# Fifteen weight tiles of the second layer split earlier and kept in DRAM, and its last convolution blocks cut into halves of tokens

## The chip, the cores and the metric

The kernel runs on one core of one Trainium2 chip. The metric is the device time of one execution in microseconds (us), given as the median of several runs. A core has engines that run beside each other, each with an in-order queue of its own: TensorE (PE, with its weight loads listed as PEld), VectorE (DVE), ScalarE (ACT), GpSimd (POOL) and SyncE (SP, which here only issues transfers between DRAM and the core's SBUF). PE's sums go into PSUM.

## The reference, cut to what matters

Two blocks of a model work on 1024 tokens with 1024 channels. The first block has two layers: layer 0 mixes an attention with a pooling over windows of 2, 4, 8 and 16 tokens; layer 1 is a gated convolution of 31 taps along the tokens, each channel by itself. The change concerns the end of layer 0 and the first part of layer 1:

```python
def even_mixer(h, w_in, sinks, pool_w, pool_scale, w_out):          # layer 0
    proj = h @ w_in
...
    ya = sliding_window_attention(q, k, v, sinks).astype(h.dtype) * jax.nn.silu(ga)
    yb = multiscale_pool(u, pool_w, pool_scale) * jax.nn.silu(gb)
    return jnp.concatenate([ya, yb], axis=-1) @ w_out

def odd_mixer(h, w_in, dw_w, dw_b, ln_g, ln_b, w_out):              # layer 1
    proj = h @ w_in
    a, b, gate = jnp.split(proj, [CONV_WIDTH, 2 * CONV_WIDTH], axis=-1)
    glu = a * jax.nn.sigmoid(b)
    conv = lax.conv_general_dilated(
        glu, dw_w.astype(glu.dtype), window_strides=(1,), padding=[(CONV_K - 1, 0)],
        dimension_numbers=('NWC', 'WIO', 'NWC'), feature_group_count=CONV_WIDTH)
    cf = conv.astype(jnp.float32) + dw_b.astype(jnp.float32)
...
    y = jax.nn.silu(cn).astype(h.dtype) * jax.nn.silu(gate)
    return y @ w_out
```

Each layer normalises its input before, and its output after, and adds it to x.

## The kernel before, in words

All products are of float32 values that are split into two parts: a high half, rounded by ACT (`hi`, L382), and a low half, the value less its high half, by DVE (`lo`, L386). A product is three matmuls: high by high, high by low, low by high. So every weight tile of 128 x 1024 (512 KB) is loaded by SP into `wf`, copied by ACT into `wh`, and subtracted by DVE into `wl` (`weights`, `wtile`). These come from the pool `stream`, which has two buffers for each name. A tile is then used for 24 matmuls on each of two chunks of 512 tokens (`project_chunk`, L425); the chunks are `c0h`/`c0l` and `c1h`/`c1l`.

`layer0_pooling` projects 4 tiles of u and 4 tiles of gates. For each group POOL sums windows, DVE and ACT make `dh` and `dl`, PE multiplies them by the small pooling weights (L1100), and DVE scales. At its end, `ahead` splits the first columns of the output product's input, and loads `wo0` and `wo1`.

`mix_out(0)` is layer 0's output product: `load_wo` (L499) brings eight tiles `wo0` to `wo7` through `wf`, each split by ACT and DVE, in the order 0, 1, 2, 3, 7, 6, 5, 4; for each block t of 128 tokens PE multiplies (`out_project`, L510) in two halves, and ACT and DVE normalise (`finish`), load and store x (L682, L714), and build the chunks of layer 1. A table `hooks` can call a function after a block t.

`layer1_conv` projects, for each block j of 128 channels, tile 8 + j (b; ACT applies a sigmoid, `sg`, L1129) and tile j (a; DVE multiplies, `glu`, L1140), then eight gate tiles (`gt`, L1192, stored to DRAM). The convolution of a block is shared out: ON_POOL[j] = 12 of the 31 taps go by ACT and POOL (ACT scales a shifted copy, `tap`, L1154, POOL adds it to `side`, L1155), the other 19 by DVE (one accumulation each, L1161, into `acc`; ACT starts it, L1159), and DVE adds both into `y` (L1164). Block 0's first half of tokens is convolved by itself (`first`), its second half and all other blocks in operations of 512 and 1024 columns. `tap` has three buffers, `acc` two, in PSUM.

Then `mix_out(1)` begins, with the class `Conv`: for each block of tokens PE transposes y (L109), DVE takes statistics, ACT normalises (`z`, L121), PE transposes back (L132), ACT applies the silu (`s`, L135), DVE multiplies by the gate, and the result is split into `yh` and `yl`.

A scheduler decides the order of the instructions on each engine, from the order in which the code asks for them and their dependences; the order printed below is what it made. Every engine works off its own order strictly.

Of the kernel before, what the change touches and what calls it, by code (L numbers as in the profile page):

```python
# [8 lines left out]
F32 = mybir.dt.float32  # L9
F32R = mybir.dt.float32r  # L10
# [5 lines left out]
S = 1024  # L16
D = 1024
NT = S // 128
KD = D // 128
# [3 lines left out]
EPS_B = 1e-5  # L23
BIG = 1e30
CONV_K = 31
ON_POOL = [12] * 8
GATES = [0] * 6 + [2000] * 2
EARLY = 0
HA, HB = 2, 5
# [302 lines left out]
class Kernel:  # L332
    def __init__(self, ctx, tc, a, out):
        self.tc, self.nc, self.a, self.out = tc, tc.nc, a, out
        self.const = ctx.enter_context(tc.tile_pool(name="const", bufs=1))
        self.stream = ctx.enter_context(tc.tile_pool(name="stream", bufs=2))
        self.small = ctx.enter_context(tc.tile_pool(name="small", bufs=4))
        edge = ctx.enter_context(tc.tile_pool(name="edge", bufs=1, side="right"))
        edge.tile([128, 56], F32, name="edge")
        self.const.tile([128, 32], F32, name="even")  # L340
        self.pp = ctx.enter_context(tc.tile_pool(name="pp", bufs=1, space=PSUM))
        self.px = {}

    def pool(self, name, side="left", bufs=1):
        g = self.tc.tile_pool(name=name, bufs=bufs, side=side, reuse_waits="tile")
# [54 lines left out]
    def weights(self, src, shape, hold=None):  # L400
# [8 lines left out]
        self.lo(l, f, h)  # L409
        return h, l  # L410

    def wtile(self, name, i, hold=None):
        return self.weights(self.a[name][i], [128, KD, 128], hold)

    def project(self, w, chunks, consume, m=128):
# [110 lines left out]
    def run(self):  # L526
# [22 lines left out]
        y = yp[1].tile([128, KD, S], F32, name="y")  # L549
        self.eps = EPS_A  # L550
        self.layer0_attention(chunks, y)
        early = self.pool("e0", "right")
        mixed = Feature(self, y)
        mixed.open(early[1])
# [2 lines left out]
        def ahead():  # L557
# [1 line left out]
            self.load_wo(early[1], a["wo0"], mixed.order[:EARLY_WO], wo)  # L559
            mixed.first(1)  # L560

        self.layer0_pooling(chunks, y, ahead)
        self.close(hp1, hp0)

        chunks, hp = self.mix_out(
            0, mixed, a["x"], self.x1, a["wo0"],
            a["post_norm"][0:1, :], a["pre_norm"][1:2, :], EPS_A, [(0, 4), (4, 8)], 0, wo=wo,
        )
        self.close(early)
        mixed = Conv(self, y)  # L570
        self.layer1_conv(chunks, y)
        self.close(*hp)
# [479 lines left out]
                )  # L1052
            nc.gpsimd.tensor_tensor(out=ym, in0=ym, in1=sg[:, c], op=ALU.mult)

    def layer0_pooling(self, chunks, y, ahead):
        nc, a = self.nc, self.a
        pb = self.pool("pool0", "right", 2)
        pool = pb[1]
        psc = pool.tile([128, 4], F32, name="psc", bufs=1)
        nc.sync.dma_start(out=psc, in_=a["psc"])  # L1060
        nc.vector.tensor_scalar(out=psc, in0=psc, scalar1=0.5, scalar2=None, op0=ALU.mult)
        cnt = pool.tile([128, 4, 16], F32, name="cnt", bufs=1)
        nc.sync.dma_start(out=cnt, in_=a["cnt"])
        pwf = pool.tile([128, 4, 128], F32, name="pwf", bufs=1)
        nc.sync.dma_start(out=pwf, in_=a["pw"])
        pwh = pool.tile([128, 4, 128], F32R, name="pwh", bufs=1)
        pwl = pool.tile([128, 4, 128], F32R, name="pwl", bufs=1)
        self.hi(pwh, pwf)
        self.lo(pwl, pwf, pwh)
        for g in (3, 2, 1, 0):  # L1070
            self.project(
                self.wtile("w0", 10 + g), chunks, lambda p, l0, n: self.scaled0(y[:, 4 + g, l0:l0 + n], p, l0, n)
            )
        for g in (3, 2, 1, 0):
            win = 2 << g
            if g == 0:
                ahead()
            sg = pool.tile([128, S], F32, tag="sg", name="sg")
            self.project(self.wtile("w0", 14 + g), chunks, lambda p, l0, n: self.silu2(pool, sg, p, l0, n))
            u = y[:, 4 + g, :]  # L1080
            w, step = u, 1
            while step < win:
                nw = pool.tile([128, S], F32, tag="win", name="win")
                nc.gpsimd.tensor_copy(out=nw[:, :step], in_=w[:, :step])
                nc.gpsimd.tensor_tensor(out=nw[:, step:], in0=w[:, step:], in1=w[:, :S - step], op=ALU.add)
                w, step = nw, 2 * step
            edge = self.small.tile([128, 16], F32, tag="edge", name="edge", bufs=2)
            nc.vector.tensor_tensor(out=edge, in0=w[:, :16], in1=cnt[:, g, :], op=ALU.mult)
            nc.vector.tensor_tensor(out=u[:, :16], in0=edge, in1=u[:, :16], op=ALU.subtract)
            nc.vector.scalar_tensor_tensor(  # L1090
                out=u[:, 16:], in0=w[:, 16:], scalar=1.0 / win, in1=u[:, 16:], op0=ALU.mult, op1=ALU.subtract
            )
            dh = pool.tile([128, S], F32R, tag="dh", name="dh")
            dl = pool.tile([128, S], F32R, tag="dl", name="dl")
            self.hi(dh, u)
            self.lo(dl, u, dh)
            for c in range(2):
                p = self.ps()
                for j, (st, mv) in enumerate(((pwh, dh), (pwh, dl), (pwl, dh))):
                    nc.tensor.matmul(out=p, lhsT=st[:, g, :], rhs=mv[:, HALF[c]], start=(j == 0), stop=(j == 2))  # L1100
                nc.vector.scalar_tensor_tensor(
                    out=u[:, HALF[c]], in0=p, scalar=psc[:, g:g + 1], in1=sg[:, HALF[c]],
                    op0=ALU.mult, op1=ALU.mult,
                )
        self.close(pb)
# [3 lines left out]
    def layer1_conv(self, chunks, y):  # L1109
# [36 lines left out]
        def conv(j, c0, n, acc, side, tap_tile):  # L1146
            glu = glus[j]
            for i in range(ON_POOL[j]):
                src, w = glu[:, c0 + i:c0 + i + n], dw[:, j, i:i + 1]
                if i == 0:  # L1150
                    nc.scalar.activation(out=side, in_=src, func=AF.Identity, scale=w, bias=dwb[:, j:j + 1])
                else:
                    tap = tap_tile()
                    nc.scalar.activation(out=tap, in_=src, func=AF.Copy, scale=w)  # L1154
                    nc.gpsimd.tensor_tensor(out=side, in0=side, in1=tap, op=ALU.add)  # L1155
            for i in range(ON_POOL[j], CONV_K):
                src, w = glu[:, c0 + i:c0 + i + n], dw[:, j, i:i + 1]
                if i == ON_POOL[j]:
                    nc.scalar.activation(out=acc, in_=src, func=AF.Copy, scale=w)  # L1159
                else:  # L1160
                    nc.vector.scalar_tensor_tensor(  # L1161
                        out=acc, in0=src, scalar=w, in1=acc, op0=ALU.mult, op1=ALU.add
                    )
            nc.vector.tensor_tensor(out=y[:, j, c0:c0 + n], in0=acc, in1=side, op=ALU.add)  # L1164
# [4 lines left out]
        def side_tile():  # L1169
            return pool.tile([128, S], F32, tag="side", name="side")  # L1170
# [26 lines left out]
            for c in HALF:  # L1197
                nc.scalar.dma_start(out=self.gates[:, j, c], in_=gt[:, c])
        xp = self.psum_pool("pxc1", "acc")
        for j in range(KD):  # L1200
            c0 = N if j == 0 else 0
            n = S - c0
            acc = xp[1].tile([128, S], F32, tag="acc", name="acc", bufs=2)
            conv(j, c0, n, acc[:, :n], side_tile()[:, :n], lambda: tap_tile()[:, :n])
        self.close(low, mid, top, xp)


# [656 lines left out]
```

## Time and profile before

| | us |
|---|---|
| median of 3 runs | 1967.2 (1966.25 to 1968.06) |
| the profiled execution | 1961.58 |
| its span, first to last instruction | 1959.8 |
| PE busy in the span | 1902.9 (97%) |
| DVE busy | 1340.1 (68%) |
| ACT busy | 905.8 (46%) |
| POOL busy | 538.3 (27%) |

The mean granted clock of PE is 0.992 of full speed over the span. The shares are means over stages that differ much: POOL is nearly idle in most of the program and full in the convolution. 1.8 us of the profiled execution lie outside the span. The profiled execution is one of its own, and is shorter than the median of the timed runs by 5.6 us.

### The profile page before, as it was taken

What the parts mean: (1) busy time and instruction counts of PE and PEld (TensorE: products, weight loads), DVE (VectorE), ACT (ScalarE), POOL (GpSimd) and SP (SyncE); (2) the same over time, 40 slices, a digit from 0 to 9 for tenths busy, and PEclk for the clock granted to TensorE, in tenths of its full rate; (3) what the DMA queues carried; (4) which work ended last, traced back from release to release, by engine and by line L of the source; (5) the groups of instructions that cost most, each with busy time, mean ns of one, the idle gap of its engine ahead of it and who ended that gap; (6) DMA issues with size and microseconds to landing.
All of it is one profiled execution on the core that took longest, in us unless ns stands there. A gap on an engine that the chain in (4) does not pass through costs nothing. (4 is left out here: it accounts for less than half of the span.)

```text
span 1959.8 us, 25557 instructions
## 1 busy us (share of the span) xinstructions
PE 1902.9 (97%) x9584; PEld 1615.4 (82%) x9584; DVE 1340.1 (68%) x2045; ACT 905.8 (46%) x1577; POOL 538.3 (27%) x433
## 2 busy tenths in 40 slices
PE   7999999899999899999999999999999999999998
PEld 6888788787778678898999999787888887888886
DVE  7788656699898565565656665657767665665666
ACT  6556234456665665555444543424333333333333
POOL 4122602479998121001010201202433230000002
PEclk9999999999999999999999999999999999999999
DMA  4110143111122642101110202522544446653654
GB/s 152 59 40 32 62 132 118 44 54 44 43 76 91 221 120 68 54 34 55 44 55 33 81 33 73 205 94 81 172 167 142 156 158 214 222 204 118 215 193 172
DMA packets 122747, 212.15 MB, mean 108 GB/s; under 512 B 9576, under 2 KB 59112, under 8 KB 122624
## 3 DMA queue, kind: packets, MB, share of 16 engines
q1 hardware_dynamic: 120320, 206.34, 31.2%
q10 hardware_dynamic: 2304, 4.20, 0.6%
q8 instruction: 75, 1.23, 0.3%
q14 instruction: 48, 0.39, 0.1%
HBM read 156.46 MB, written 54.03 MB: 107 GB/s over the span
## 5 line engine op out<-in xcount | busy, mean ns | idle before, releaser
L1155 POOL TENSOR_TENSOR side<-side,tap 128x1024 f32<-128x1024 f32 (+1 forms) x99 | 235.6, 2386 | 24.9 <-ACT tap L1154 17.8
L1161 DVE SCALAR_TENSOR_TENSOR acc<-glu,dw,acc 128x1024 f32<-128x1024 f32 (+1 forms) x162 | 193.9, 1239 | 11.5 <-ACT acc L1159 10.2
L425 PE MATMUL pj<-c0h,wl 128*128 128x512 f32 (+1 forms) x496 | 187.9, 379 | 5.7 <-DVE wl L386 5.7
L425 PE MATMUL pj<-c0h,wh 128*128 128x512 f32 (+1 forms) x496 | 189.1, 381 | 4.2 <-ACT gt L1192 2.7
L425 PE MATMUL pj<-c0l,wh 128*128 128x512 f32 (+1 forms) x496 | 187.6, 378 | 0.0
L425 PE MATMUL pj<-c1h,wh 128*128 128x512 f32 (+1 forms) x496 | 176.5, 356 | 3.6 <-ACT sg L1129 1.8
L425 PE MATMUL pj<-c1l,wh 128*128 128x512 f32 (+1 forms) x496 | 177.1, 357 | 0.0
L425 PE MATMUL pj<-c1h,wl 128*128 128x512 f32 (+1 forms) x496 | 176.8, 357 | 0.0
L1154 ACT ACTIVATE tap<-glu,dw 128x1024 f32<-128x1024 f32 (+1 forms) x99 | 103.8, 1055 | 78.9 <-POOL side L1155 78.4
L382 ACT ACTIVATE ah<-act 128x1024 fp32r<-128x1024 f32 x56 | 59.2, 1060 | 168.4 <-issue 82.2
L386 DVE TENSOR_TENSOR al<-act,ah 128x1024 fp32r<-128x1024 f32 x56 | 68.5, 1225 | 90.7 <-ACT ah L382 90.6
L382 ACT ACTIVATE ph<-pt 128x512 fp32r<-128x512 f32 (+3 forms) x144 | 72.8, 516 | 104.8 <-PE pt L1461 68.3
L386 DVE TENSOR_TENSOR pl<-pt,ph 128x512 fp32r<-128x512 f32 (+3 forms) x144 | 83.3, 587 | 41.0 <-ACT ph L382 40.6
L425 PEld LDWEIGHTS pj<-c0h,wl 128*128 128x128 f32 x496 | 94.1, 190 | 19.0 <-DVE wl L386 6.1
L425 PEld LDWEIGHTS pj<-c0h,wh 128*128 128x128 f32 x496 | 94.1, 190 | 18.3 <-ACT gt L1192 3.1
L425 PEld LDWEIGHTS pj<-c1h,wh 128*128 128x128 f32 x496 | 94.2, 190 | 17.9 <-ACT sg L1129 2.3
L386 DVE TENSOR_TENSOR wl<-wf,wh 128x1024 fp32r<-128x1024 f32 (+1 forms) x66 | 90.7, 1374 | 23.4 <-ACT wh L382 23.2
L425 PEld LDWEIGHTS pj<-c1l,wh 128*128 128x128 f32 x496 | 94.3, 190 | 13.0 <-DVE c1l L386 0.4
L425 PEld LDWEIGHTS pj<-c1h,wl 128*128 128x128 f32 x496 | 94.5, 190 | 12.3
L425 PEld LDWEIGHTS pj<-c0l,wh 128*128 128x128 f32 x496 | 93.9, 189 | 12.6 <-issue 0.2
L1715 PE MATMUL pd<-bh,ah 128*128 128x512 f32 x256 | 99.3, 392 | 3.4 <-ACT ah L382 3.4
L1715 PE MATMUL pd<-bl,ah 128*128 128x512 f32 x256 | 100.4, 392 | 0.0
(607 smaller groups left out, 5103.0 us busy)
## 6 DMA issues: line engine op xcount, KB each, us to landing
wf<-in_w SPq DMA_DIRECT2D x63, 512.0 KB, 3.5
raw<-in_ff SPq DMA_DIRECT2D x32, 512.0 KB, 4.6
act<-acts SPq DMA_DIRECT2D x32, 512.0 KB, 3.3
w<-in_ff SPq DMA_DIRECT2D x32, 512.0 KB, 4.4
acts<-s SPq DMA_DIRECT2D x48, 256.0 KB, 3.6
act<-act SPq DMA_DIRECT2D x24, 512.0 KB, 3.4
wf<-in_wo SPq DMA_DIRECT2D x20, 512.0 KB, 3.8
cb<-cum SPq DMA_DIRECT2D x8, 520.0 KB, 3.6
```

Source lines behind the costliest of these rows:

```text
L382: self.nc.scalar.activation(out=out, in_=src, func=AF.Copy, scale=scale)
L386: return self.nc.vector.tensor_tensor(out=out, in0=src, in1=hi.bitcast(F32), op=ALU.subtract)
L425: self.nc.tensor.matmul(out=p[:m, :n], lhsT=st[:, k, :], rhs=mv[:, k, :], start=(k == 0 and j == 0), stop=(k == KD - 1 and j == 2),)
L1154: nc.scalar.activation(out=tap, in_=src, func=AF.Copy, scale=w)
L1155: nc.gpsimd.tensor_tensor(out=side, in0=side, in1=tap, op=ALU.add)
L1161: nc.vector.scalar_tensor_tensor(out=acc, in0=src, scalar=w, in1=acc, op0=ALU.mult, op1=ALU.add)
L1715: nc.tensor.matmul(out=bank, lhsT=st[:, k, c], rhs=mv[:, k, :], start=(fresh and first and j == 0), stop=(last and j == 2), skip_group_che ...
```

## The change

Three things are changed. First, 15 of layer 1's 24 weight tiles (tiles 8 + j and j for all j, but tile 7) are split ahead of time by `split_ahead`: loaded into `af` (one buffer), split into `ah` and `al`, and both halves stored to DRAM tiles. It is called eight times in `layer0_pooling`, after each projection, and seven times from `mix_out(0)`, as the hook of t = 1 to 7. `wtile` then loads the two halves of such a tile straight into `wh` and `wl`, without ACT and DVE. The tile 7 and the eight gate tiles go the old way. Second, ON_POOL falls from 12 to 11 for blocks 4 to 7. Third, blocks 6 and 7 are convolved together by halves of tokens: block 6 first half, block 7 first half, block 6 second half, block 7 second half.

```diff
-ON_POOL = [12] * 8
+ON_POOL = [12] * 4 + [11] * 4
...
+    def split_ahead(self, name, i):
+
+        f = self.ahead.tile([128, KD, 128], F32, tag="f", name="af")
+        h, l = (self.ahead.tile([128, KD, 128], F32R, tag=t, name="a" + t) for t in "hl")
+        self.nc.sync.dma_start(out=f, in_=self.a[name][i])
+        self.hi(h, f)
+        self.lo(l, f, h)
+        parts = [self.tc.dram_tile([128, KD, 128], F32, name=f"{name}{t}{i}") for t in "hl"]
+        for d, t in zip(parts, (h, l)):
+            self.nc.sync.dma_start(out=d, in_=t.bitcast(F32))
+        self.parts[name, i] = parts
+
     def wtile(self, name, i, hold=None):
+        if (name, i) in self.parts:
+            ws = [self.stream.tile([128, KD, 128], F32R, tag=t, name=t) for t in ("wh", "wl")]
+            for w, d in zip(ws, self.parts.pop((name, i))):
+                self.nc.sync.dma_start(out=w.bitcast(F32), in_=d)
+            return ws
         return self.weights(self.a[name][i], [128, KD, 128], hold)
...
+        pre = self.pool("ahead", "right")
+        self.ahead = pre[1]
+        tiles = [t for j in range(KD) for t in (KD + j, j)]
+
+        def split_next(*_):
+            self.split_ahead("w1", tiles.pop(0))
+
...
-        self.layer0_pooling(chunks, y, ahead)
+        self.layer0_pooling(chunks, y, ahead, split_next)
...
+            hooks={t: split_next for t in range(1, NT)},
         )
-        self.close(early)
+        self.close(early, pre)
...
                 self.wtile("w0", 10 + g), chunks, lambda p, l0, n: self.scaled0(y[:, 4 + g, l0:l0 + n], p, l0, n)
             )
+            split_next()
...
             self.project(self.wtile("w0", 14 + g), chunks, lambda p, l0, n: self.silu2(pool, sg, p, l0, n))
+            split_next()
...
-        for j in range(KD):
-            c0 = N if j == 0 else 0
-            n = S - c0
-            acc = xp[1].tile([128, S], F32, tag="acc", name="acc", bufs=2)
-            conv(j, c0, n, acc[:, :n], side_tile()[:, :n], lambda: tap_tile()[:, :n])
+        for js, halves in [((j,), [HALF[1] if j == 0 else slice(0, S)]) for j in range(KD - 2)] + [((KD - 2, KD - 1), HALF)]:
+            accs = {j: (xp[1].tile([128, S], F32, tag="acc", name="acc", bufs=2), side_tile()) for j in js}
+            for c in halves:
+                for j in js:
+                    acc, side = (t[:, c] for t in accs[j])
+                    n = c.stop - c.start
+                    conv(j, c.start, n, acc, side, lambda: tap_tile()[:, :n])
```

On ACT, where layer 0's pooling ends and its output product begins (`th` is the sigmoid part of a pooling gate, `dh` the pooled group, `yh` the split input of the output product), stood before:

```order
L968 ACTIVATE th<-pr 128x512
L382 ACTIVATE dh<-y 128x1024
L968 ACTIVATE th<-pr 128x512 x4
L382 ACTIVATE wo2h<-wf 128x1024
L382 ACTIVATE wo3h<-wf 128x1024
L382 ACTIVATE yh<-y 128x512
L382 ACTIVATE wo7h<-wf 128x1024
L382 ACTIVATE yh<-y 128x512
L382 ACTIVATE wo6h<-wf 128x1024
L382 ACTIVATE yh<-y 128x512
L382 ACTIVATE wo5h<-wf 128x1024
L382 ACTIVATE wo4h<-wf 128x1024
```

The same place on ACT after the change (L993 is the line of `th` there):

```order
L993 ACTIVATE th<-pr 128x512
L382 ACTIVATE ah<-af 128x1024
L993 ACTIVATE th<-pr 128x512
L382 ACTIVATE yh<-y 128x512
L382 ACTIVATE ah<-af 128x1024
L382 ACTIVATE wo2h<-wf 128x1024
L382 ACTIVATE wo3h<-wf 128x1024
L382 ACTIVATE yh<-y 128x512 x2
L382 ACTIVATE ah<-af 128x1024
L382 ACTIVATE wo7h<-wf 128x1024
L382 ACTIVATE yh<-y 128x512
L382 ACTIVATE wo6h<-wf 128x1024
```

Copies of tiles for layer 1 now stand ahead of `wo2h` and ahead of `wo7h`, and one more ahead of `wo5h`.

On SP, the transfers issued at that place; before, between the load of the last layer-0 tile and those of the first layer-1 tiles, there were these (`wf` numbered 2662 to 2682 are `wo2`, `wo3`, `wo7`, `wo6`, `wo5`, `wo4`):

```order
L402 DMA wf_2542<-in_w0 128x1024
L499 DMA wf_2662<-in_wo0 128x1024
L499 DMA wf_2666<-in_wo0 128x1024
L397 DMA gpre_2690<-in_pre_norm 128x1024
L397 DMA gpost_2692<-in_post_norm 128x1024
L499 DMA wf_2670<-in_wo0 128x1024
L499 DMA wf_2674<-in_wo0 128x1024
L682 DMA y_155<-in_x 128x8x128
L499 DMA wf_2678<-in_wo0 128x1024
```

After the change, from the first pair `wh`, `wl` that is read from DRAM to the load of `wo7` (`wf_2753`); the loads of `wo2` and `wo3` stand earlier:

```order
L428 DMA wh_3607<-w1h8_2074 128x1024
L428 DMA wl_3608<-w1l8_2075 128x1024
L421 DMA w1l10_2356<-al_2351 128x1024
L416 DMA af_2456<-in_w1 128x1024
L421 DMA w1h2_2462<-ah_2457 128x1024
L421 DMA w1l2_2463<-al_2458 128x1024
L416 DMA af_2560<-in_w1 128x1024
L428 DMA wh_3611<-w1h0_2142 128x1024
L428 DMA wl_3612<-w1l0_2143 128x1024
L707 DMA y_155<-in_x 128x8x128
L397 DMA gpre_2773<-in_pre_norm 128x1024
L421 DMA w1h11_2566<-ah_2561 128x1024
```

Behind these come `gpost`, the store of `w1l11`, the load of the next `af`, and then `wo7`. 18 transfers stand in the queue between the loads of `wo3` and `wo7`, where there were two.

On DVE, where the convolution of block 0 begins (`c1l` is the low half of the second chunk, `acc_3520` the accumulator of block 0's first half of tokens), stood before:

```order
L1161 SCALAR_TENSOR_TENSOR acc_3520<-glu,dw,acc_3520 128x512
L1140 TENSOR_TENSOR glu<-pj,sg 128x512
L1161 SCALAR_TENSOR_TENSOR acc_3520<-glu,dw,acc_3520 128x512
L386 TENSOR_TENSOR wl<-wf,wh 128x1024
L1161 SCALAR_TENSOR_TENSOR acc_3520<-glu,dw,acc_3520 128x512 x3
L1161 SCALAR_TENSOR_TENSOR acc<-glu,dw,acc 128x512
```

The same place after the change, from block 0's first accumulation:

```order
L1188 SCALAR_TENSOR_TENSOR acc_3670<-glu,dw,acc_3670 128x512
L386 TENSOR_TENSOR c1l<-pd,c1h 128x4x128
L1188 SCALAR_TENSOR_TENSOR acc_3670<-glu,dw,acc_3670 128x512 x11
L1167 TENSOR_TENSOR glu<-pj,sg 128x512
L1188 SCALAR_TENSOR_TENSOR acc_3670<-glu,dw,acc_3670 128x512 x5
L1188 SCALAR_TENSOR_TENSOR acc<-glu,dw,acc 128x512
```

The subtractions `wl` are gone from between the accumulations; the second `glu` of block 0 still stands behind eleven or twelve of these.

## Rows read from the trace of the kernel before

**Rows 1.** Windows: PE, PEld, DVE, ACT, POOL busy; PE clock, DMA share, GB/s

```profile
216.00:267.00 51.00, 49.38 (x216) 39.99 (x215) 39.33 (x45) 13.89 (x18) 25.17 (x17) 1.00 0.19 63
267.00:330.00 63.00, 63.00 (x296) 52.50 (x295) 40.04 (x48) 29.45 (x57) 11.89 (x28) 1.00 0.52 159
...
580.00:630.00 50.00, 50.00 (x223) 41.22 (x222) 47.74 (x40) 29.83 (x33) 47.92 (x18) 1.00 0.28 100
630.00:660.00 30.00, 23.52 (x103) 18.67 (x102) 11.83 (x16) 12.64 (x22) 2.90 (x9) 0.89 0.55 177
```

**Rows 2.** Waits of PE, 300–420 and 420–660: total us, times, longest

```profile
PE pj L425 <- DVE wl L386: 5.7, 1, 5.7
...
PE pj L425 <- ACT gt L1192: 2.7, 1, 2.7
...
PE pj L425 <- ACT sg L1129: 1.8, 1, 1.8
PE pj L425 <- DVE glu L1140: 1.4, 1, 1.4
```

**Rows 3.** PE in short stretches: busy us, matmuls, granted clock, DMA share, GB/s

```profile
393.00:397.00 4.00, 3.98 (x11) 0.63 0.39 131
461.10:466.00 4.90, 4.86 (x21) 1.00 0.00 2
501.50:505.00 3.50, 3.44 (x9) 0.54 0.41 124
566.40:570.00 3.60, 3.56 (x9) 0.54 0.19 73
```

**Rows 4.** Groups by line in 376–646: count, busy us, mean ns, idle before

```profile
L1155 POOL TENSOR_TENSOR side<-side,tap 128x1024 f32<-128x1024 f32 x77 | 201.4, 2622 | 13.6 <-ACT tap L1154 7.9 <-ACT side L1151 1.0
L1161 DVE SCALAR_TENSOR_TENSOR acc<-glu,dw,acc 128x1024 f32<-128x1024 f32 x126 | 155.0, 1280 | 10.3 <-ACT acc L1159 9.7
L1154 ACT ACTIVATE tap<-glu,dw 128x1024 f32<-128x1024 f32 x77 | 88.4, 1151 | 72.0 <-POOL side L1155 71.5 <-ACT gt L1192 0.4
...
L1161 DVE SCALAR_TENSOR_TENSOR acc<-glu,dw,acc 128x512 f32<-128x512 f32 x36 | 38.9, 1095 | 1.2 <-ACT acc L1159 0.5
...
L386 DVE TENSOR_TENSOR wl<-wf,wh 128x1024 fp32r<-128x1024 f32 x22 | 34.6, 1572 | 3.8 <-ACT wh L382 3.8
```

**Rows 5.** Timeline of POOL and DVE: start, length, instruction, count

```profile
450.84 19.12 POOL L1155 TENSOR_TENSOR side<-side,tap 128x1024 f32<-128x1024 f32 x7
...
550.10 7.37 POOL L1155 TENSOR_TENSOR side<-side,tap 128x1024 f32<-128x1024 f32 x3
...
569.16 59.86 POOL L1155 TENSOR_TENSOR side<-side,tap 128x1024 f32<-128x1024 f32 x22 [0.98 <-ACT side L1151]
...
392.89 0.74 DVE L1161 SCALAR_TENSOR_TENSOR acc<-glu,dw,acc 128x512 f32<-128x512 f32 x1
...
455.70 1.21 DVE L386 TENSOR_TENSOR wl<-wf,wh 128x1024 fp32r<-128x1024 f32 x1
...
466.32 1.38 DVE L386 TENSOR_TENSOR wl<-wf,wh 128x1024 fp32r<-128x1024 f32 x1
```

**Rows 6.** Timeline of PE at the end of the gates

```profile
647.42 0.66 PE L132 MATMUL pj<-ident,z 128*128 128x128 f32 x4 [1.87 <-ACT z L121]
...
653.89 1.22 PE L510 MATMUL pd<-wo0h,yh 128*128 128x512 f32 x2 [4.50 <-ACT yh L382]
```

**Rows 7.** Timeline of DVE in the pooling

```profile
229.48 2.03 DVE L386 TENSOR_TENSOR dl<-y,dh 128x1024 fp32r<-128x1024 f32 x1 [1.13 <-ACT dh L382]
```

**Rows 8.** Timeline of ACT and PE at the start of layer 0's output product

```profile
267.10 1.05 ACT L382 ACTIVATE wo2h<-wf 128x1024 fp32r<-128x1024 f32 x1
...
272.38 1.07 PE L510 MATMUL pd<-wo2h,yh 128*128 128x512 f32 x4
```

**Rows 9.** Transfers: the page's queue, and issues in 200–340 with us to landing

```profile
q1 hardware_dynamic: 120320, 206.34, 31.2%
...
wf<-in_wo SPq DMA_DIRECT2D x8, 512.0 KB, 3.5
```

More of the change, by code (lines that the diff above doesn't have):

```diff
@@ L341, in __init__ @@
         self.pp = ctx.enter_context(tc.tile_pool(name="pp", bufs=1, space=PSUM))
-        self.px = {}
+        self.px, self.parts = {}, {}
     def pool(self, name, side="left", bufs=1):
@@ L1053, in attend0, with layer0_pooling @@
             nc.gpsimd.tensor_tensor(out=ym, in0=ym, in1=sg[:, c], op=ALU.mult)
-    def layer0_pooling(self, chunks, y, ahead):
+    def layer0_pooling(self, chunks, y, ahead, split_next):
         nc, a = self.nc, self.a
```

## The prediction

> **What bounds the kernel now.** I read the windows by stage first. TensorE (PE) works nearly all the time nearly everywhere: in the 580–630 us stretch 223 matmuls fill 50.00 us, so a 512-column matmul at full clock costs 0.224 us [rows 1]. A change gains only where PE idles or runs at the lower clock. Layer 1's projection and convolution (about 374 to 645 us) has such places, and the waits of PE name them [rows 2]: 5.7 us for a weight's low half (DVE wl), 2.7 us for ACT's gt, 1.8 us for ACT's sg, 1.4 us for DVE's glu. Each is one event. The granted clock behind them is the second thing to read [rows 3]: after the wl wait 0.63 in 393–397, after the sg wait 0.54 in 501.5–505, after the gt wait 0.54 in 566.4–570, but 1.00 after the 1.4 us wait (461.1–466). So each of the three longer waits also costs a stretch near 1.2 GHz instead of 2.4: 4.0 x 0.37 = 1.5 us, 3.5 x 0.46 = 1.6 us and 3.6 x 0.46 = 1.7 us. Together the three are worth 5.7 + 1.5 + 1.8 + 1.6 + 2.7 + 1.7 = 15.0 us. That is the most that this stage can give by these events.
>
> Who makes PE wait? The lines of the stage [rows 4] and the windows [rows 1] show POOL (47.92 of 50 us) and DVE (47.74 of 50 us) both full in 580–630. ACT stood 71.5 us before its 1024-wide taps waiting for POOL's side adds, so ACT's in-order queue moves at POOL's pace, and an sg or gt behind a tap comes late. POOL's adds are not all alike [rows 5]: three beside DVE taps whose accumulator is in PSUM take 7.37 us, 2.46 each; the seven from 450.84 take 19.12 us, and into those fall two wl splits (455.70 and 466.32): (19.12 - 7 x 2.46) / 2 = 0.95 us more for each.
>
> The last place is the seam into layer 1's output product. PE ends its gates at 645.55 (647.42 less a wait of 1.87) and starts wo0 at 653.89, with a few transposes between [rows 6].
>
> **The change, part by part.**
>
> *Splits taken out of the convolution.* 15 of layer 1's 24 weight tiles lose their ACT copy and DVE subtraction at their use. The tile that PE waited for 5.7 us now arrives as two loads. 22 of the 24 subtractions lie in the stage (those of block 0 come ahead of it), and 9 tiles keep theirs, so 13 go: 13 x 1.572 = 20.4 us on DVE [rows 4]. Four of the 13 (blocks 1 and 2) lie ahead of POOL's 1024-wide adds; the other 9 no longer lengthen an add, 9 x 0.95 = 8.6 us on POOL.
>
> *Four taps to DVE.* DVE gains 4 x 1.28 = 5.1 us, POOL loses 4 x 2.46 = 9.8 us, two of the four taps (blocks 4 and 5) before the gt wait at 566.
>
> *Blocks 6 and 7 by halves.* 38 of DVE's 1024-wide taps become 76 of 512. The 512-wide cost is bounded by 0.64 (half of 1.28) and 1.095 us (the mean beside POOL's lock-step) [rows 4]; the one at 392.89, 0.74 us [rows 5], is nearest in kind, since its neighbours are DVE's own. 76 x 0.74 - 38 x 1.28 = +7.6 us (bounds 0 and +34.6). DVE's balance over the stage is -20.4 + 5.1 + 7.6 = -8 us.
>
> So POOL reaches the gt wait with up to 8.6 + 4.9 = 13 us less work behind it, and PE no longer meets wl. But sg, gt and glu keep their place behind taps in in-order queues. In DVE's order eleven 512-wide taps still stand ahead of block 0's second glu, only wl is gone from among them. I expect three short waits of 1.3 us (like the 1.4 us one, without a fall of clock) instead of the three long ones: 15.0 - 3 x 1.3 = **11 us gained** (5 if only wl's 7.2 less 1.3 goes and the rest stays; 14 if nearly nothing comes back). The gates then end near 634.5. The convolution ended about when POOL did, 569.16 + 59.86 = 629.0 [rows 5] and a y sum; with 8 us less on DVE near 625, still before the gates' end, so it does not set the seam. The seam itself stays: ACT's order around it is the same row by row (gt, z, wo0h, wo1h, s, yh), and I count nothing for the earlier start of the transposes.
>
> *What the moved work costs in the pooling and in layer 0's output product.* PE has 1.6 us idle in 216–267, and none in 267–330 [rows 1]. Anything late there is lost outright.
>
> First DVE. It is busy 39.33 of 51 us in 216–267 and gets some seven more subtractions. Their price beside POOL's window sums lies between 1.2 us (a split in the convolution, [rows 5]) and 2.03 us (dl at 229.48, [rows 7]): 8 to 14 us into 11.7 us of slack. ACT's additional copies are 7 x 1.05. I put 2 us of delay on pooled groups (bounds 0 and 3); a few wo0 and wo1 matmuls drawn forward cover some of it.
>
> The second cost is ACT's queue. Before, wo2h runs at 267.10 and PE first uses it at 272.38 [rows 8]: 5.3 us of cover. After, two ah copies stand ahead of wo2h, and each waits for an af load. There is one af buffer, so a load can be issued only when the al before it has run. Transfers: the queue moved 206.34 MB in 31.2% of 16 engines' span [rows 9], 337 GB/s, so 1.55 us per 512 KB in a row; a lone load lands after 3.5 us, 1.95 us more. The first wh/wl pair from DRAM takes the buffer of the last but one layer-0 tile, which comes free when the last one starts, 48 x 0.224 = 10.8 us before its end at about 265.5 (272.38 less 30 matmuls): 254.7. From there: wh, wl, w1l10 and af, 4 x 1.55 + 1.95, lands at 263; ah and al until about 265.5; w1l2 and the next af, 2 x 1.55 + 1.95, lands at 270.5; ah, then wo2h at about 272.7, then wo2l. PE is there at 272.4. The wait would be near 1 us by this chain, and near 4 us if the bursts on SP (stores, wh, wl, y, gpre) put the af back by 3 us more. I take 2.4 us and a slow stretch of 1.6 us, as in [rows 3]. Next is wo7h, behind an af that eleven transfers precede: 265.5 + 11 x 1.55 = 282.6, wo7h at 284.7; PE wants it after 24 matmuls of wo2 and wo3 and 24 of t=2 drawn forward, 272.4 + 10.8 + 4 = 287. Covered, by 2 us. wo5h has more. **Loss: 2 + 2.4 + 1.6 = 6 us** (1 to 9).
>
> The transfers themselves: 45 more of 512 KB, 45 x 1.55 = 70 us of the 16 engines, mostly between 216 and 345. The share there is 0.19 and then 0.52 [rows 1]; it would come near to full, which hides only as long as nothing in the queue is urgent.
>
> At this point a rule speaks against the change. The row dl at 229.48 [rows 7] shows a DVE subtraction of 2.03 us beside POOL's sums, so it is lengthened there. The Trainium skill (SBUF — State Buffer, "SBUF: two separate sides") says that a DVE instruction with two SBUF inputs and a GpSimd instruction that reads SBUF take a port pair exclusively for the whole instruction, and that the other blocks fully. By that rule a subtraction that meets an add waits for all of it, and the time would be 1965 (rival E). The row agrees with a block of part of an add only, and the sum goes by the row.
>
> **Sum.** Against the profiled execution (1961.58 us, span 1959.8): -11 + 6 = -5 us, 1956.6. That execution lies 5.6 us under the median of the runs, 1967.2, so the median after is 1967.2 - 5 = **1962**.
>
> **The rivals.**
> A (forecast, 0.42): gain 11, loss 4 to 8, net -3 to -8: 1959 to 1964.
> B (0.22), the pooling hides its new work: af loads land before ACT comes to them, loss 0 to 2, gain 11 to 14: 1953 to 1958. For it: DVE's 11.7 us of slack, ACT busy only 13.89 of 51 us [rows 1]. Against: the one af buffer and SP's in-order queue.
> C (0.15), slower: the ah copies ahead of wo2h, wo7h and wo5h hold ACT's queue while their loads stand in the burst. If a transfer costs 2.1 instead of 1.55 us when loads and stores run together, wo7h comes 11 x 0.55 = 6 us later, 4 us beyond its cover, and wo5h again; with the slow clock after each and the 6 us of the forecast this is a loss of 13 to 19 us against 11: +2 to +8, 1969 to 1975. It decides from a loss of 11 us on. For it: the share of DMA; against: t=2's matmuls as cover.
> D (0.14), the convolution does not speed up: DVE's balance of -8 us is gone if a half tap costs 0.85; then glu, and PE behind it, keep DVE's old pace: gain 2 to 5, loss 3 to 5: -3 to +3, 1964 to 1970.
> E (0.07), the moved subtractions wait for whole adds of POOL in the pooling. POOL is busy half of 216–267 (25.17 of 51 us [rows 1]); half of seven subtractions at 2.46 + 1.2, half at 1.2 make 17 us into 11.7 of slack, 5 us late instead of 2: loss 9, net -2, 1965. For it: dl's 2.03; against: that it is not 3.7.
>
> **Numbers.** A measurement can tell about 0.2%, 3.9 us, from no change. Faster by more: A 0.29 and B 0.22, 0.51. Same: A 0.13, C 0.05, D 0.12, E 0.04, 0.34. Slower: C 0.10, D 0.02, E 0.03, 0.15. The range 1952 to 1974 holds A, B, D, E and most of C.
>
> **What would show it.** Right: no wl wait in layer 1's projection; fewer POOL adds above 3 us; gates' end 11 us closer to the stage's start; PE waiting a few us for wo2h, and DMA share near 0.9 in 267–330; the seam still 8 us. Wrong: a wait of PE on wo7h or wo5h (C); no wait at all before 330 (B); gt still waited for, with DVE full to the gates' end (D). A stall in the pooled groups of over 5 us would speak for E.

## The result, and the profile after

The changed kernel takes 1977.13 us (1975.08 to 1978.31, 4 runs), the kernel before 1966.72 us beside it: ratio 1.0062, 95% interval 1.005 to 1.0074. It is slower, where 1962 was forecast.

To see where, I cut both profiled executions by four events in PE's timeline: A from the last attention matmul of layer 0 to the first matmul on layer 1's second chunk (pooling, output product, start of layer 1); B to the last gate matmul; C to the first matmul on the third chunk of the projection behind it (the next output product); D from there to PE's last matmul. Before: A 164.6, B 271.3, C 146.8, D 1158.9 us. After: A +16.0, B -9.1, C +5.0, D +1.1, and 1.5 us in the start ahead of A, which the change does not touch. That is 14.5 of the 15.2 us between the two profiled executions (1976.73 and 1961.58). The medians lie 10.4 apart, since the profiled execution of before is one of its short ones, and which stage it owes that to is not known. Each stage below is read from one execution per kernel. The start ahead of A, where PE has the same order in all kernels, differed by -1.0 to +3.6 us, and a stage A that no edit touched by up to 1.4 us; a stage difference of that size says little.

The windows of after by stage, columns as in [rows 1]:

```profile
216.00:267.00 51.00, 46.66 (x203) 37.54 (x202) 43.88 (x46) 18.19 (x21) 26.23 (x19) 1.00 0.55 194
267.00:330.00 63.00, 53.71 (x225) 43.29 (x225) 32.65 (x37) 26.10 (x42) 7.85 (x13) 0.95 0.90 314
```

Where PE had 63.00 of 63 us it has 53.71, and DMA share is 0.90. The waits of PE in 216–420 and, last row, 420–660 answer to [rows 2]:

```profile
PE pj L442 <- DVE glu L1167: 7.2, 1, 7.2
PE pd L527 <- ACT wo2h L382: 5.4, 1, 5.4
PE pd L527 <- DVE pt L538: 3.6, 1, 3.6
PE ps L1127 <- ACT dh L382: 3.3, 1, 3.3
...
PE ps L1127 <- DVE dl L386: 1.0, 2, 0.6
PE pj L442 <- DMA wh<-w1h: 0.8, 1, 0.8
...
PE pj L442 <- ACT gt L1219: 0.2, 1, 0.2
```

Before, 216–300 had one such wait:

```profile
PE ps L1100 <- ACT dh L382: 1.5, 1, 1.5
```

And short stretches of PE after the change, columns as in [rows 3]; the first three lie behind the waits for wo2h, pt and glu, the last two in stage C:

```profile
282.30:286.00 3.70, 3.67 (x10) 0.61 1.07 281
315.40:319.00 3.60, 3.60 (x10) 0.57 0.95 295
411.00:415.00 4.00, 3.45 (x8) 0.51 0.00 0
662.20:668.00 5.80, 5.80 (x17) 0.55 0.62 224
674.00:680.00 6.00, 5.71 (x22) 0.72 0.67 222
```

Most of stage A's loss adds up from these. dh and dl cost 3.3 + 1.0 against 1.5 before: 2.8. wo2h costs 5.4 and 3.7 x 0.39 = 1.4 by the granted clock: 6.8. pt, the normalising of the first token block, which frees PSUM for the fourth, costs 3.6 and 3.6 x 0.43 = 1.5: 5.1. That is 14.7 of 16.0 us. In stage B the sg wait is gone and gt's is 0.2, but where PE waited 5.7 us for wl it now waits 7.2 us for glu.

ACT's timeline shows why wo2h is late:

```profile
262.33 1.06 ACT L382 ACTIVATE ah<-af 128x1024 fp32r<-128x1024 f32 x1 [1.57 <-DMA af<-in_w]
...
273.10 1.06 ACT L382 ACTIVATE ah<-af 128x1024 fp32r<-128x1024 f32 x1 [4.28 <-DMA af<-in_w]
...
280.27 1.06 ACT L382 ACTIVATE ah<-af 128x1024 fp32r<-128x1024 f32 x1 [2.93 <-DMA af<-in_w]
281.23 1.04 ACT L382 ACTIVATE wo2h<-wf 128x1024 fp32r<-128x1024 f32 x1
```

and SP's timeline the loads for these three copies, with a store and the first reload between them:

```profile
257.38 0.42 SPq L416 DMA_DIRECT2D af<-in_w  x1
...
263.42 0.32 SPq L421 DMA_DIRECT2D w1h<-ah  x1
263.84 0.38 SPq L428 DMA_DIRECT2D wh<-w1h  x1
...
265.61 0.38 SPq L416 DMA_DIRECT2D af<-in_w  x1
...
275.82 0.45 SPq L416 DMA_DIRECT2D af<-in_w  x1
```

From 237 us on each lap of the single af buffer (load, copy, subtraction, next load) takes 7 to 11 us, and wo2h, 1 us of work on a tile whose load SP issued at 240.94, stands behind the last lap: 281.23 instead of 267.10 [rows 8].

### The profile page after: what moved, and what is told of

Its sections match the earlier page's. It is cut to its first block, busy times and chain, and to the rows that moved or that the text cites. A ratio compares the mean times of both kernels' runs of the same rounds, so it can differ in the third digit from the quotient of the medians.

```text
span 1974.6 us, 25767 instructions
## 1 busy us (share of the span) xinstructions
PE 1906.6 (97%) x9584; PEld 1618.1 (82%) x9584; DVE 1348.1 (68%) x2089; ACT 909.3 (46%) x1597; POOL 523.5 (27%) x449
## 5 line engine op out<-in xcount | busy, mean ns | idle before, releaser
L1182 POOL TENSOR_TENSOR side<-side,tap 128x512 f32<-128x512 f32 (+1 forms) x115 | 219.0, 1911 | 25.1 <-ACT tap L1181 17.4
L1188 DVE SCALAR_TENSOR_TENSOR acc<-glu,dw,acc 128x512 f32<-128x512 f32 (+1 forms) x204 | 202.7, 1041 | 11.3 <-ACT acc L1186 9.2
L1181 ACT ACTIVATE tap<-glu,dw 128x512 f32<-128x512 f32 (+1 forms) x115 | 104.3, 918 | 59.8 <-POOL side L1182 59.2
L442 PEld LDWEIGHTS pj<-c0l,wh 128*128 128x128 f32 x496 | 93.5, 189 | 12.6 <-issue 0.2
L1744 PE MATMUL pd<-bh,al 128*128 128x512 f32 x256 | 100.0, 393 | 0.0
```

The source lines that it names most:

```text
L442: self.nc.tensor.matmul(out=p[:m, :n], lhsT=st[:, k, :], rhs=mv[:, k, :], start=(k == 0 and j == 0), stop=(k == KD - 1 and j == 2),)
L1188: nc.vector.scalar_tensor_tensor(out=acc, in0=src, scalar=w, in1=acc, op0=ALU.mult, op1=ALU.add)
L1744: nc.tensor.matmul(out=bank, lhsT=st[:, k, c], rhs=mv[:, k, :], start=(fresh and first and j == 0), stop=(last and j == 2), skip_group_che ...
```

## The experiments

All changes of a stage are against the kernel before, ratios with their 95% interval.

| kernel | A | B | C | D | median us | ratio |
|---|---|---|---|---|---|---|
| the change | +16.0 | -9.1 | +5.0 | +1.1 | 1977.13 | 1.0062 (1.005 to 1.0074) |
| ahead_only | +15.6 | -7.8 | +3.8 | +0.7 | 1974.78 | 1.0056 (1.004 to 1.0072) |
| no_ahead | +1.4 | -2.0 | +2.5 | +0.3 | 1963.32 | 0.9993 (0.9983 to 1.0004) |
| transfers_only | +4.8 | -9.2 | +3.8 | -0.1 | 1963.62 | 0.9994 (0.9984 to 1.0004) |
| splits_only | +12.9 | -2.4 | +4.8 | +6.3 | 1986.38 | 1.0109 (1.0093 to 1.0125) |
| no_stores | +13.3 | -0.4 | +4.5 | 0.0 | 1978.71 | 1.0073 (1.0061 to 1.0086) |
| pooling_only | +14.1 | -5.5 | +3.8 | -0.4 | 1974.96 | 1.0054 (1.0041 to 1.0067) |
| two_loads | +15.6 | -7.7 | +4.4 | -0.1 | 1971.0 | 1.0032 (1.0022 to 1.0043) |
| seven_free | +9.6 | -3.8 | +0.4 | +0.9 | 1969.43 | 1.0021 (1.0012 to 1.003) |
| seven_behind | +2.9 | -4.9 | +5.8 | +6.7 | 1975.53 | 1.0049 (1.0035 to 1.0062) |
| acc_psum | +18.3 | -15.0 | +4.1 | -0.4 | 1968.62 | 1.0015 (1.0005 to 1.0025) |
| psum_two_loads | +15.4 | -16.2 | +1.2 | -0.1 | 1962.11 | 0.999 (0.9981 to 0.9999) |
| before_acc_psum | -0.1 | -10.6 | 0.0 | +0.6 | 1952.66 | 0.9932 (0.992 to 0.9944) |
| rest_acc_psum | +1.4 | -13.7 | +1.6 | +0.6 | 1951.14 | 0.9934 (0.9922 to 0.9947) |
| seven_behind_psum | +4.5 | -12.6 | +4.6 | +8.9 | 1966.59 | 1.001 (1.0001 to 1.0019) |

### Which part

Each half of the change by itself. ahead_only is the changed kernel with these two taken back (the loop over blocks as a whole), no_ahead the kernel before with these two alone:

```diff
-ON_POOL = [12] * 4 + [11] * 4
+ON_POOL = [12] * 8
...
-        for js, halves in [((j,), [HALF[1] if j == 0 else slice(0, S)]) for j in range(KD - 2)] + [((KD - 2, KD - 1), HALF)]:
+        for j in range(KD):
```

> The early splits alone, with 12 taps on POOL everywhere and whole blocks. Where the loss sits in the pooling and layer 0's output product, the first matmul on the second chunk comes 17 us later than before, as in the changed kernel (391.4 against 373.9). The stage after it: if the missing weight subtractions free POOL, the sg and gt waits are short and the gates end 4 to 9 us earlier relative to that point; if the taps moved to DVE gave that gain, the gt wait of 2.7 us is still there and the gain is under 3 us. Whole time +8 to +14 us against before; by my forecast's sum, which this tests a second time, it would be -2.

> The four taps on DVE and the halves of tokens, without the early splits. First theory (the early splits carry the whole loss): nothing changes before 374 us, the wl wait of 5.7 us stays, the gt wait shrinks, time -4 to 0 us. Rival (the halves disturb the seam to the next output product, which lost 5 us in the changed kernel): the same 5 us are lost after the gates, time +1 to +6 us.

The early splits alone carry the loss of stage A and most of the gain of B. Taps and halves are worth 2.0 us in B and lose 2.5 in C, both near what an untouched stage differs by; the time is the same within 0.2%.

### What in the early splits

transfers_only leaves the arithmetic out and stores f twice; splits_only works on one tile that stays in SBUF, without the 15 loads, the stores and the reloads; no_stores keeps the 15 loads and drops the stores and the reloads. The edits in split_ahead, in this order (splits_only also loses the stores, as in the third edit; its tile, resident, is loaded once):

```diff
-        self.hi(h, f)
-        self.lo(l, f, h)
...
-        for d, t in zip(parts, (h, l)):
-            self.nc.sync.dma_start(out=d, in_=t.bitcast(F32))
+        for d, t in zip(parts, (f, f)):
+            self.nc.sync.dma_start(out=d, in_=t)
```

```diff
-        f = self.ahead.tile([128, KD, 128], F32, tag="f", name="af")
+        f = self.resident
...
-        self.nc.sync.dma_start(out=f, in_=self.a[name][i])
```

```diff
-        for d, t in zip(parts, (h, l)):
-            self.nc.sync.dma_start(out=d, in_=t.bitcast(F32))
-        self.parts[name, i] = parts
```

> The early work without its arithmetic: af is loaded and stored twice to DRAM, no copy on ACT and no subtraction on DVE, so that layer 1 uses unsplit weights in both halves. Theory Q (ACT's queue stands behind copies that wait for an af load): the 17.5 us of loss up to the second chunk fall to 6 or less, with no wait for wo2h. Theory B (the transfers crowd out the wo and x loads): 12 us or more stay.

> The early work without its transfers: 15 copies on ACT and 15 subtractions on DVE of a tile that stays in SBUF, nothing stored, and layer 1 splits its weights at their use as before. Theory Q: the loss up to the second chunk is 0 to 4 us. Theory P (added work on DVE and ACT, lengthened beside POOL's sums, makes the pooled groups late): 8 us or more.

> The changed kernel with its 15 early loads, copies and subtractions, but without the 30 stores and the 30 loads from DRAM; layer 1 splits all its tiles at their use, so the early work is done for nothing. One af buffer, as in the changed kernel, and copies ahead of wo2h in ACT's order too. Theory Q (copies at the head of ACT's queue wait for a load that can't be issued sooner): the second chunk begins 10 us or more late, PE waits for wo2h 3 us or more, though the queue of transfers is far from full. Theory B (the stores and reloads crowd the loads out): less than 5 us late, no wait for wo2h.

The transfers alone cost 4.8 us in stage A, with a DMA share of 0.87 in 267–330: most of it is hidden, as forecast. The splits without any transfer cost 12.9 us, against my number for theory Q (0 to 4) and within theory P's (8 or more). But that kernel is a poor separation. With no load to wait for, the scheduler put all 15 copies ahead of wo2h, and they waited all the same, each for the subtraction before it: ACT stood idle for 24.8 us there. So copies that wait at the head of ACT's queue are in this kernel too. It also shows subtractions lengthened beside POOL's sums. The groups by line in 205–290 us of splits_only, then of after:

```profile
L386 DVE TENSOR_TENSOR al<-af,ah 128x1024 fp32r<-128x1024 f32 x15 | 23.5, 1568 | 2.1 <-ACT ah L382 2.1
...
L382 ACT ACTIVATE ah<-af 128x1024 fp32r<-128x1024 f32 x15 | 15.9, 1060 | 25.0 <-DVE al L386 24.8
```

```profile
L386 DVE TENSOR_TENSOR al<-af,ah 128x1024 fp32r<-128x1024 f32 x7 | 12.2, 1742 | 9.2 <-ACT ah L382 9.2
```

A subtraction takes 1.57 and 1.74 us in the mean, instead of 1.21 [rows 5]. no_stores speaks for Q: no store, no reload, and yet PE's wait and the loads' time to landing read

```profile
PE pd L523 <- ACT wo2h L382: 5.7, 1, 5.7
```

```profile
af<-in_w SPq DMA_DIRECT2D x14, 512.0 KB, 3.5
```

With the DMA share at 0.33 and 0.61 in 216–267 and 267–330, a load lands in 3.5 us, and PE still waits 5.7 us for wo2h. What all kernels with a stage A over 9 us late share is copies ahead of wo2h in ACT's order; transfers_only and, below, seven_behind have none.

pooling_only loses the hooks, two_loads gets a second buffer for af:

```diff
-            hooks={t: split_next for t in range(1, NT)},
```

```diff
-        f = self.ahead.tile([128, KD, 128], F32, tag="f", name="af")
+        f = self.ahead.tile([128, KD, 128], F32, tag="f", name="af", bufs=2)
```

> The changed kernel without the hooks: eight tiles are split early, the other seven at their use as before. If the seven splits of the output product carry the part of the loss behind wo2 (some 7.6 us), the second chunk begins about 7 us earlier than in the changed kernel; the convolution gives back 2 to 4 us of its gain, since seven subtractions return to it. 1970 to 1975. If the loss up to wo2 alone decides (dh, wo2h), less than 3 us is won before the second chunk and the time is 1975 to 1980.

> The changed kernel with two af buffers instead of one, so that a load can be issued before the subtraction of the tile ahead has run. Theory Q (ACT's queue stands behind copies that wait for loads which were issued too late): the wait for wo2h falls from 5.4 to under 2 us, and the second chunk begins 4 to 9 us earlier than in the changed kernel, which gives 1967 to 1973. Theory P (the added subtractions and copies themselves): the second chunk moves by less than 2 us, 1975 to 1978.

Eight tiles cost nearly as much as fifteen: the loss does not go in step with the number. A second buffer shortened the wait for wo2h to 2.6 us, but the scheduler then put nine copies ahead of it instead of seven, PE waited 3.0 us elsewhere in the pooling, and the second chunk began only 2.2 us earlier, between the numbers of both theories. The median fell by 6 us, of which this profile shows under 3; where the rest went is open.

### The place, tested with the work held fixed

Seven tiles, asked for by the hooks only (the two calls of split_next in layer0_pooling are gone, and the list of tiles begins at its third). In seven_free the scheduler still puts all seven copies ahead of wo2h. seven_behind adds one edge (last_wo is the copy of the last tile that load_wo brings, wo4h):

```diff
-        self.hi(h, f)
+        with self.tc.issue_after(self.last_wo.ins):
+            self.hi(h, f)
```

> The changed kernel with seven early tiles instead of fifteen (9, 1, 10, 2, 11, 3, 12), asked for by the hooks alone; no calls in the pooling. The scheduler nevertheless places all seven copies ahead of wo2h on ACT, from the pooling on. If their place in the queues costs the time, the second chunk begins 8 us or more late, nearly as with eight or fifteen, although the code asks for them after the output product has begun; time 1970 to 1976. If the number of the splits and transfers costs it, half of it is gone: 1965 to 1970.

> The same seven tiles with one edge more: each copy stands behind wo4h in ACT's order. The work, the transfers and the one af buffer are the same. If the place in the queues costs the time, there is no wait for wo2h, the second chunk begins 0 to 4 us late, and the time is 6 to 12 us less than with the seven placed freely: 1961 to 1966. If the amount of work or transfers costs it, the second chunk is as late as with these.

The waits of PE up to the second chunk, seven_free and then seven_behind:

```profile
PE pd L527 <- ACT wo2h L382: 3.7, 1, 3.7
PE ps L1125 <- ACT dh L382: 3.3, 1, 3.3
```

```profile
PE ps L1126 <- ACT dh L382: 1.5, 1, 1.5
...
PE pd L528 <- ACT wo7h L382: 0.6, 1, 0.6
```

The same copies, subtractions and transfers, and stage A falls from +9.6 to +2.9 us; dh is back at the 1.5 us of the kernel before. seven_free itself is 9.6 us late, as the place predicts, at a time (1969.4) that I had put down to the number; for fifteen tiles A is 16.0, so the number counts too, from a high start. The place is shown to be the larger part for seven tiles; for fifteen it is argued from there. The edge moves whole laps out of the pooling, with their subtractions beside POOL's sums, so this run alone does not tell the place in ACT's order from the place in DVE's.

The time missed its expectation all the same, by other stages. In D, PE waits 5.5 us in layer 2's output product for yh, where it waited 0.6 before. The wait in seven_behind, and ACT's timeline there, before and then in seven_behind (s21h is a copy for the products of the next block, of sums that POOL makes):

```profile
PE ps L528 <- ACT yh L382: 5.5, 1, 5.5
```

```profile
1243.83 1.09 ACT L382 ACTIVATE yh<-pj 128x512 fp32r<-128x512 f32 x2 [3.48 <-PE pj L161]
1248.17 1.06 ACT L382 ACTIVATE s21h<-sums 128x1024 fp32r<-128x1024 f32 x1 [3.25 <-POOL sums L220]
```

```profile
1254.47 1.06 ACT L382 ACTIVATE s21h<-sums 128x1024 fp32r<-128x1024 f32 x1 [7.47 <-POOL sums L220]
1255.44 1.06 ACT L382 ACTIVATE yh<-pj 128x512 fp32r<-128x512 f32 x2
```

The scheduler has put s21h ahead of yh, far from anything edited, and yh stands behind a copy that waits 7.5 us for POOL: the same fault as with wo2h. Of all kernels here s21h stands ahead of these yh in splits_only, seven_behind and seven_behind_psum alone, and these are the three that lose over 6 us in D.

### The wait for glu

```diff
-            conv(0, 0, N, half("acc0"), half("side0"), lambda: half("tap0", 2))
+            conv(0, 0, N, xp[1].tile([128, S], F32, tag="acc", name="acc0", bufs=2)[:, :N], half("side0"), lambda: half("tap0", 2))
```

(xp, the pool in PSUM, is opened ahead of it.) Three kernels further below combine this with the parts tried so far: rest_acc_psum with no_ahead, psum_two_loads with two_loads; seven_behind_psum with seven_behind.

> The changed kernel with one edit: block 0's first accumulator lies in PSUM instead of SBUF; the order of DVE's instructions stays the same row by row up to block 0's second glu. Theory L (with the accumulator in SBUF a tap of DVE has two SBUF inputs and waits for POOL's adds, 1.48 us instead of 0.74; that makes glu late, and PE waited for it 7.2 us, where wl was waited for before): taps of 0.7 to 0.8 us, the wait for glu is gone or under 1 us, its slow clock too, time 6 to 9 us less than the changed kernel, 1968 to 1971. Rival (glu waits for ACT's sg or for the projection itself): taps get shorter, the wait stays over 4 us.

> The kernel before with the same one edit: block 0's first accumulator in PSUM. By theory L the wait of 5.7 us for wl had the same cause, since wl stood behind ten such taps: the wait falls under 1.5 us, and the time is 4 to 8 us less than before. By the reading of my forecast (wl is late because its own copy and subtraction come late): the wait stays near 5 us, the time within 2 us of before.

DVE's timeline of after, and then of acc_psum:

```profile
394.66 16.24 DVE L1188 SCALAR_TENSOR_TENSOR acc<-glu,dw,acc 128x512 f32<-128x512 f32 x11
410.81 0.68 DVE L1167 TENSOR_TENSOR glu<-pj,sg 128x512 f32<-128x512 f32 x1
```

```profile
395.11 8.67 DVE L1188 SCALAR_TENSOR_TENSOR acc<-glu,dw,acc 128x512 f32<-128x512 f32 x11 [0.56 <-ACT acc L1186]
404.34 0.69 DVE L1167 TENSOR_TENSOR glu<-pj,sg 128x512 f32<-128x512 f32 x1 [0.56 <-PE pj L442]
```

The same eleven taps ahead of glu take 1.48 us each with the accumulator in SBUF and 0.79 in PSUM; the wait for glu is gone, and what is left there is 2.3 us for wh's load. In the kernel before, such taps stood ahead of wl. Its timeline of DVE, and that of before_acc_psum:

```profile
377.13 14.70 DVE L1161 SCALAR_TENSOR_TENSOR acc<-glu,dw,acc 128x512 f32<-128x512 f32 x9
391.76 1.21 DVE L386 TENSOR_TENSOR wl<-wf,wh 128x1024 fp32r<-128x1024 f32 x1
```

```profile
376.32 7.09 DVE L1161 SCALAR_TENSOR_TENSOR acc<-glu,dw,acc 128x512 f32<-128x512 f32 x9 [0.50 <-ACT acc L1159]
385.30 1.23 DVE L386 TENSOR_TENSOR wl<-wf,wh 128x1024 fp32r<-128x1024 f32 x1 [1.89 <-ACT wh L382]
```

A rival would be that PSUM is the faster place by itself. The kernel before answers it. POOL's timeline there:

```profile
376.27 9.98 POOL L1155 TENSOR_TENSOR side<-side,tap 128x512 f32<-128x512 f32 x6 [0.21 <-ACT tap L1154]
386.51 4.77 POOL L1155 TENSOR_TENSOR side<-side,tap 128x512 f32<-128x512 f32 x3 [0.26 <-ACT tap L1154]
395.78 1.40 POOL L1155 TENSOR_TENSOR side<-side,tap 128x512 f32<-128x512 f32 x1 [4.49 <-ACT tap L1154]
```

The tap at 392.89 [rows 5] has its accumulator in SBUF too, but falls where POOL is idle (391.28 to 395.78), and takes 0.74 us; the nine beside POOL's adds take 1.63 each. So it takes both, the accumulator in SBUF and POOL's adds beside it.

The waits of PE in before_acc_psum, 300–420 and 420–640:

```profile
PE pj L425 <- ACT c1h L382: 1.6, 1, 1.6
...
PE pj L425 <- ACT gt L1194: 2.4, 4, 1.1
...
PE pj L425 <- ACT sg L1129: 1.2, 3, 0.7
```

No wait for wl, no wait over 1.1 us for sg or gt. Both expectations of theory L held, the second by more than was put down (12 us instead of 4 to 8). POOL's adds of block 0 are faster too (eight in 10.87 us from 373.59, against six in 9.98), and the later waits for sg and gt are short; that the one makes the other is argued, not tested. One line gives 10.6 us in stage B, more than the change with all its transfers (9.1), and costs nothing elsewhere.

> The kernel before with block 0's first accumulator in PSUM, the four taps on DVE and the halves of tokens, without early splits. If the taps and halves add to the accumulator's 12 us, the time is 1946 to 1951; if the convolution is no longer what PE waits for once the accumulator lies in PSUM, it is 1952 to 1956, since the seam to the next product then loses some 2 us by its changed order.

> The changed kernel with both edits: the accumulator in PSUM and two af buffers. If each takes away its own part (8.5 us and 6 us of 12), 1961 to 1966: level with the kernel before, and 9 us or more behind the kernel before with the accumulator in PSUM alone. If the two buffers only seemed to help, 1967 to 1971.

> The seven tiles behind wo4h, and block 0's first accumulator in PSUM. If both losses are then gone and the early splits still give the convolution something, 1946 to 1951, better than the kernel before with the accumulator in PSUM (1952.7). If PE no longer waits for anything in the convolution that the splits could take away, 1952 to 1957: the accumulator is then the whole gain, and the early splits are worth nothing even where they cost little.

With the accumulator in PSUM, taps and halves bring B to -13.7 but nothing in time, and early splits take the kernel back to where it began: psum_two_loads as expected, seven_behind_psum above both of its ranges, for 8.9 us in D, in the same place as seven_behind. before_acc_psum and rest_acc_psum are the versions that beat both kernels, by 0.68% and 0.66% over the one before, which is no difference between them.

## Why the prediction was wrong, step by step

**The loss in stage A** is the step that failed: "Loss: 2 + 2.4 + 1.6 = 6 us", measured 16.0. Its terms: pooled groups 2 us, measured 2.8; wo2h "near 1 us by this chain", taken as 2.4 and 1.6, measured 5.4 and 1.4. The chain of transfers was begun at a layer-0 buffer that comes free at 254.7, as if nothing stood ahead of wh in SP's order. But the store w1h did, and it waited for a copy of the lap before, at 262.33: SP issued wh at 263.84, 9.1 us late. From there the chain ran much as worked out: 17.4 us to wo2h at 281.23, where I had 18.0; the copy that I had at about 264 ran at 273.10. One has to count a single buffer's laps from the first one.

"Covered, by 2 us. wo5h has more": PE waited for neither, but not for the reason given. wo7h ran at 292.73, not at 284.7, and PE was late itself. The sum ended there, and the 5.1 us for pt come behind it, which I did not see at all. PE had three blocks of tokens open and took each new wo tile to all three; wo4h, the last tile, ran at 304.81 (before at 284.1), the three ended together near 311.6, and PE then stood until the first was normalised. The wait is 3.6 us with fifteen tiles, 2.3 with eight (wo4h at 302.39) and none with seven (seven_free, 294.71). That wo4h's lateness makes it is read from these traces, not tested.

**"three short waits of 1.3 us"** in stage B: sg's vanished, gt's is 0.2 us, and in wl's place stand 7.2 us for glu. My step read the row "PE waits for wl" as the cost of wl, and not as that of what stood ahead of wl on DVE; [rows 4] had it, 512-wide taps at 1.095 us in the mean against 0.74 for one [rows 5]. The other half held: the 9 subtractions were to take 8.6 us off POOL's 1024-wide adds, and ahead_only, with the same 77 of them, has 192.2 us against 201.4 [rows 4], and no wait for gt over 0.2. Its group of adds in 393–652:

```profile
L1182 POOL TENSOR_TENSOR side<-side,tap 128x1024 f32<-128x1024 f32 x77 | 192.2, 2507 | 13.8 <-ACT tap L1181 9.2
```

That the gain came to 9.1 of the 11 forecast is in part luck. Behind the wait of 1.6 us for c1h, which both kernels have at the start of B, the granted clock was 0.66 in the kernel before and 1.00 in the changed one. That is 5.0 x 0.34 = 1.7 us of the gain that no step had counted (columns as in [rows 3], before and then after):

```profile
373.90:378.90 5.00, 5.00 (x14) 0.66 0.00 0
391.40:396.40 5.00, 5.00 (x21) 1.00 0.00 0
```

**"ACT's order around it is the same row by row"**: true for the rows that I listed, which end at yh. Behind yh, wo2h had changed places with two z and a group of s. ACT's timeline of before, and then of after:

```profile
653.21 0.63 ACT L382 ACTIVATE yh<-s 128x512 fp32r<-128x512 f32 x1 [1.89 <-DVE s L139]
654.58 1.06 ACT L382 ACTIVATE wo2h<-wf 128x1024 fp32r<-128x1024 f32 x1 [0.74 <-DMA wf<-in_wo]
```

```profile
661.48 0.63 ACT L382 ACTIVATE yh<-s 128x512 fp32r<-128x512 f32 x1 [1.42 <-DVE s L139]
663.24 0.78 ACT L121 ACTIVATE z<-ps,lnb,lrs 128x512 f32<-128x512 f32 x1 [1.13 <-POOL lnb L118]
...
665.95 1.07 ACT L382 ACTIVATE wo2h<-wf 128x1024 fp32r<-128x1024 f32 x1
```

PE then waited 2.0 us for wo4h, with the clock at 0.72 in 674–680: stage C lost 5.0 us where I counted nothing. That this order causes it is argued, not tested. All kernels with it lost 3.8 to 5.8 us in C; those with before's order lost 0 to 2.5, but two_loads, which has before's order too, lost 4.4.

**The rivals.** C named the mechanism (copies ahead of the wo tiles in ACT's queue), with 0.15, but put what it added to the forecast at wo7h and wo5h, and its 1969 to 1975 ends below the measured time. E, subtractions that wait beside POOL's sums, added little: 1.74 us for a subtraction in the pooling is between my bounds. What E weighed on the moved subtractions decided elsewhere, on the taps already there: 1.48 us with two inputs in SBUF beside POOL's adds, 0.79 with one of them in PSUM. The Trainium skill (SBUF — State Buffer, "Who interferes with whom") says that a DVE instruction contends with GpSimd's reads when it has two SBUF inputs and, outside its two-port modes, not with one. The runs agree with it on these taps.

## What to carry to other kernels

A row that says what PE waits for names the last instruction of a queue; price the whole of what stands ahead of it there before you remove it, or the wait will only change its name. Work that is moved under a busy engine is paid for by its place in the in-order queues: with one staging buffer, count the laps of load, copy and subtraction from the first, see which urgent instruction stands behind the last, and do the same for SP, where a store that waits for a copy holds up the loads behind it. An edit can also turn an order far away, as s21h and yh show, so read the stages that it does not touch. Where DVE and POOL work side by side, an operand in PSUM in place of SBUF can be worth more than a reordering: here 12 us for one line.

## What I had not expected of the hardware

A fused multiply-add of DVE with 512 columns takes 0.79 us (mean of eleven in a row) with its accumulator in PSUM and 1.48 us with it in SBUF, both while GpSimd adds beside it, so nearly twice for the same arithmetic; with it in SBUF and GpSimd idle it took 0.74. And in transfers_only the transfers took 0.63 and 0.87 of the DMA engines' time in 216–267 and 267–330, where they had 0.19 and 0.52 [rows 1]; that alone made stage A only 4.8 us longer, with the engines' splits left out.
